# A two-layer encoder's seam between MLP and latent attention: a scratch pool of its own, two tiles' transposes moved among the latent products, and later weight splits tied to a later point

## The chip, the cores and the metric

The kernel runs on one core of one Trainium2 chip. The metric is the device time of one execution in microseconds, the median of several runs. A profile of one more execution gives the trace that is quoted here; times in it count from the start of its span.

## The reference

A bidirectional encoder of two layers works on 512 positions of width 1024 in float32. Each layer is x = x + mixer(norm(x)) followed by x = x + MLP(norm(x)). The MLP is squared ReLU, 1024 to 4096 to 1024. Layer 0's mixer is dilated window attention (A), layer 1's is multi-head latent attention (B):

```
lat = h @ w_in                                   # 1024 -> 256 + 128 + 64
q  = (rms_norm(lat[:256], g) @ w_qb)             # 8 heads of 128 + 64 (rotary)
kv = (rms_norm(lat[256:384], g) @ w_kvb)         # 8 heads of 128 (key) + 128 (value)
k  = concat(kv key part, lat[384:448] for all heads)
q, k = rms_norm per head, rotary on the last 64
y  = softmax(q k^T / sqrt(192)) v, all positions; then y @ w_o
```

The document is about the seam: the end of layer 0's MLP, the norm after it, the product `h @ w_in` ("the latents") and the first per-head products, up to the first attention scores.

## The kernel before

**Precision by splitting.** Every float32 product is made of three passes of a faster format: an operand x is split into a high part (ScalarE copies x to the short format, tile `whi` or the like) and a low part (VectorE computes x minus the high part, `wlo`). The product is high*high + high*low + low*high. So each weight tile costs a ScalarE instruction and a VectorE instruction before TensorE can use it, and so does each activation tile that TensorE has transposed.

**Tiles of positions.** The 512 positions are four tiles r = 0 to 3 of 128. The normed activations stand transposed in `hT` (eight blocks of 128 channels, high and low). A tile's path at the seam is in `norm_tile`: ScalarE squares and sums (L138), GpSimd raises to the power -1/2 (L133), VectorE multiplies by the row factor and by the gain table `g_mix` (L224, result `xn`), and then `turn` has TensorE transpose eight blocks in two halves (L125, tile `tp`), ScalarE write the high part into `hT` (L234) and VectorE the low part (L235).

**The end of the MLP** (`mlp`, `wino`) adds its products into `resid`. When both halves of a tile r are added, `done0(r, c)` is called and makes that tile's norm. Scratch there lives in the pool `mlp0`, where the pool's big tiles are the MLP's activations (`a2`) and sums (`S`); `xn` is in the same pool with tag `S`.

**The latents.** `run_block(w_units(b_w_in[0], 0, 448), [4], 448, ...)` makes, for each r in turn, 24 matmuls of 448 columns (four weight units u of two channel blocks, three passes) into the PSUM tile `acc` of that r. When a tile r is complete, `evac_lat(r, acc)` follows: three squares with sums on ScalarE into the scratch `junkb`, the power on GpSimd, VectorE's products with the gain table `gl` (result `cn`, L1009 and L1010), the rotary part, three transposes on TensorE into a `tp` tile, and `cT`, high by ScalarE (L1022), low by VectorE (L1023).

**The pairs.** The eight heads are worked in four pairs. `new_pair(p)` loads the pair's two weights (tile `raw`, three buffers, shared with all other weight loads) and splits them. `kv_chunk(d, r)` and `q_chunk(d, r)` project tile r of `cT`, evacuate, and return a second part that transposes the result. After the latents, the kernel runs the kv chunks of pair 0 and its first q chunk, then a loop of `score` steps into which later chunks are woven.

**What sets the order.** The kernel is written in the order above, but a scheduler that estimates times places each engine's instructions; each engine then runs its own list strictly in that order, and an instruction that waits holds up all that stand behind it. `tc.issue_after(ins)` adds an edge: what is created inside the block stands behind `ins` on the same engine. Loads are issued from SP's list, in its order. A tag with one buffer (the gain table's tag `gain` in pool `gp`, which holds `g_mix`, then `gl`, then `g_ffn`) makes the load of the next one wait until the last reader of the one before is done. PSUM tiles `tp` have two buffers.

`block_groups` has a hook that the MLP already uses: `between={i: f}` calls f after step i of the block; f's transposes stand behind step i's last matmul, and step i+1 stands behind f's last transpose. In the latents, step i is tile r = i // 4 and weight unit i % 4.

## Time and profile before

| | us |
|---|---|
| median of 3 runs | 1405.03 (1404.77 to 1405.65) |
| the profiled execution | 1405.79 |
| its span, first to last instruction | 1404.0 |
| TensorE busy in the span | 1371.9 (98%) |
| VectorE busy | 940.9 (67%) |
| ScalarE busy | 801.2 (57%) |
| GpSimd busy | 225.3 (16%) |
| mean granted TensorE clock | 0.999 |

In the views below, PE is TensorE, DVE VectorE, ACT ScalarE, POOL GpSimd and SPq the list from which SP issues loads. A row of the timeline has the start in us, the length in us, the engine, the line, the operation, the tiles (out<-in, buffer numbers left out), the shape, how many instructions were merged, and in brackets how long the engine was idle just before and what ended that. A length given for several merged matmuls is from the first one's start to the last one's end; matmuls overlap, so the step from one to the next is shorter than one's length.

The seam lies between 842 us (the last products of the MLP) and 904 us (the first score). The four latents run from 865.69 to 888.35 us, the first kv products start at 888.73 us, the first score matmul at 903.69 us, and the attention lasts until about 1005 us.

### The profile page before, as it was taken

What the parts mean: (1) busy time and instruction counts of PE and PEld (TensorE: products, weight loads), DVE (VectorE), ACT (ScalarE), POOL (GpSimd) and SP (SyncE); (2) the same over time, 40 slices, a digit from 0 to 9 for tenths busy, and PEclk for the clock granted to TensorE, in tenths of its full rate; (3) what the DMA queues carried; (4) which work ended last, traced back from release to release, by engine and by line L of the source; (5) the groups of instructions that cost most, each with busy time, mean ns of one, the idle gap of its engine ahead of it and who ended that gap; (6) DMA issues with size and microseconds to landing.
All of it is one profiled execution on the core that took longest, in us unless ns stands there. A gap on an engine that the chain in (4) does not pass through costs nothing.

```text
span 1404.0 us, 18978 instructions
## 1 busy us (share of the span) xinstructions
PE 1371.9 (98%) x6852; PEld 1164.1 (83%) x6852; DVE 940.9 (67%) x1498; ACT 801.2 (57%) x1643; POOL 225.3 (16%) x240
## 2 busy tenths in 40 slices
PE   7999999999999999999999999999999999999998
PEld 6999878888889989888888878777769888888886
DVE  6885777788788744574655769788745465574747
ACT  6543778687786625454536455777534553644543
POOL 1110212121122001020200204433201020020101
PEclk9999999999999999999999999999999999999999
DMA  9535554655555539486583944201116668493835
GB/s 301 172 133 162 131 135 98 164 124 133 143 125 123 159 106 260 142 187 176 121 238 86 235 96 94 61 31 31 46 46 191 170 132 228 100 226 124 200 85 120
DMA packets 171775, 197.83 MB, mean 141 GB/s; under 512 B 59105, under 2 KB 109025, under 8 KB 171681
## 3 DMA queue, kind: packets, MB, share of 16 engines
q1 hardware_dynamic: 152496, 157.55, 37.9%
q0 software_dynamic: 19184, 39.07, 15.5%
q8 instruction: 54, 0.88, 0.3%
q14 instruction: 41, 0.33, 0.1%
HBM read 176.13 MB, written 7.86 MB: 131 GB/s over the span
## 4 chain that ended last, share of the span: by engine, by line
PE 81%; DVE 7%; ACT 4%; DMA 4%; issue 2%; SPq 0%; POOL 0%; ACTq 0%; DVEq 0%
PE acc L188 46%; PE sc L868 11%; PE tp L868 7%; PE tp L125 3%; DMA xT<-t 2%; PE sc L430 2%; PE acc L1161 1%; PE sc L1055 1%; DVE wlo L811 1%; PE acc L1137 1%; PE tp L430 1%; PE sco L710 1%; PE acc L430 1%; PE sco L706 1%; ACT junk L138 1%
## 5 line engine op out<-in xcount | busy, mean ns | idle before, releaser
L188 PE MATMUL acc<-whi,hT 128*128 128x512 f32 (+2 forms) x1208 | 377.2, 388 | 1.9 <-ACT hT L752 1.0
L188 PE MATMUL acc<-hT_f,whi 128*128 128x512 f32 (+1 forms) x1152 | 317.4, 366 | 0.0
L159 DVE TENSOR_TENSOR wlo<-raw,whi 128x1024 fp32r<-128x1024 f32 (+3 forms) x146 | 172.9, 1188 | 164.3 <-ACT whi L158 163.7
L188 PEld LDWEIGHTS acc<-whi,hT 128*128 128x128 f32 x1208 | 224.3, 188 | 43.0 <-ACT hT L1163 1.5
L158 ACT ACTIVATE whi<-raw 128x1024 fp32r<-128x1024 f32 (+3 forms) x146 | 149.6, 1029 | 161.8 <-PE acc L188 72.1
L188 PEld LDWEIGHTS acc<-hT_f,whi 128*128 128x128 f32 x1152 | 207.8, 189 | 34.9
L188 PE MATMUL acc<-wlo,hT 128*128 128x512 f32 (+2 forms) x604 | 233.0, 387 | 0.7 <-DVE wlo L159 0.7
L811 DVE TENSOR_TENSOR wlo<-wqs,whi 128x1024 fp32r<-128x1024 f32 x112 | 137.7, 1231 | 112.9 <-ACT whi L810 112.9
L810 ACT ACTIVATE whi<-wqs 128x1024 fp32r<-128x1024 f32 x112 | 118.3, 1059 | 161.6 <-PE acc L188 65.0
L188 PE MATMUL acc<-hT_f,wlo 128*128 128x512 f32 (+1 forms) x576 | 204.1, 366 | 0.0
L868 PE MATMUL sc<-whi,asp 128*128 128x512 f32 x512 | 165.2, 390 | 1.3 <-DVE resid L842 1.3
L796 POOL DMA_DIRECT2D wqs<-in_ffn_w_dram x64 | 77.6, 1347 | 540.1 <-DVE wlo L811 358.3
L188 PEld LDWEIGHTS acc<-wlo,hT 128*128 128x128 f32 x604 | 113.6, 188 | 20.2 <-DVE wlo L159 1.1
L188 PEld LDWEIGHTS acc<-hT_f,wlo 128*128 128x128 f32 x576 | 108.3, 189 | 17.4
L868 PEld LDWEIGHTS sc<-whi,asp 128*128 128x128 f32 x512 | 96.2, 188 | 21.9 <-issue 2.1
L868 PE MATMUL tp<-whi,asp 128*128 128x512 f32 x352 | 112.2, 390 | 0.9 <-DVE resid L842 0.9
L133 POOL TENSOR_TENSOR qrs<-rs_v,nhalf 128x4 f32<-128x4 f32 x48 | 65.9, 1376 | 264.1 <-DVE rs_v L130 233.2
L868 PE MATMUL sc<-wlo,asp 128*128 128x512 f32 x256 | 99.7, 390 | 0.0
L304 ACT ACTIVATE qkT<-xT 128x1024 uint16<-128x1024 uint16 x48 | 56.4, 1182 | 42.1 <-DMA xT<-t 42.0
L868 PEld LDWEIGHTS tp<-whi,asp 128*128 128x128 f32 x352 | 66.1, 188 | 15.0 <-DVE resid L842 1.3
L868 PE MATMUL tp<-wlo,asp 128*128 128x512 f32 x176 | 68.2, 390 | 0.0
L138 ACT ACTIVATE junk<-acc 128x128 f32<-128x128 f32 x192 | 52.1, 272 | 10.7 <-PE acc L188 7.0
(236 smaller groups left out, 2187.2 us busy)
## 6 DMA issues: line engine op xcount, KB each, us to landing
wqs<-in_ffn_w_dram SPq DMA_DIRECT2D x80, 512.0 KB, 5.2
raw<-in_ffn_w_dram SPq DMA_DIRECT2D x64, 512.0 KB, 4.2
wqs<-in_ffn_w_dram POOLq DMA_DIRECT2D x64, 512.0 KB, 7.5
raw<-in_a_w_qkv_dram SPq DMA_DIRECT2D x96, 256.0 KB, 3.2
b<-in_a_w_qkv_dram SPq DMA_DIRECT2D x24, 384.0 KB, 5.7
vall<-vo POOLq DMA_DIRECT2D x24, 192.0 KB, 2.3
raw<-in_a_w_o_dram SPq DMA_DIRECT2D x8, 512.0 KB, 3.8
raw<-in_b_w_o_dram SPq DMA_DIRECT2D x8, 512.0 KB, 3.8
```

Of the source, the lines that this page charges most:

```text
L125: return PE.transpose(o, i, ident)
L133: G.tensor_tensor(out, v[:, :n], nhalf[:, :n], op=ALU.pow)
L138: A.activation(junk, x, AF.Square, scale=1.0 / math.sqrt(dim), accum_out=out)
L158: A.activation(hi[:, :nk, :n], raw[:, :nk, :n], AF.Copy)
L159: V.tensor_tensor(lo[:, :nk, :n], raw[:, :nk, :n], hi[:, :nk, :n].bitcast(F32), op=ALU.subtract)
L188: last = PE.matmul(accs[o][:, oc], lhsT=lt, rhs=rt, start=(kt == 0 and p_i == 0 and hv == 0), stop=(kt == total - 1 and p_i == 2), skip_gr ...
L304: A.activation(dst, xT.rearrange("p (h c) t -> p c t h", h=2), AF.Copy)
L430: PE.matmul(banks[t][:, :VH], lhsT=lt, rhs=rt[:, j], start=(first and k == 0 and i_ == 0), stop=(k == 3 and i_ == 2), skip_group_check=True)
L796: marks["sum"] = nc.gpsimd.dma_start(t, src, accum_op=ALU.add).ins
L810: A.activation(hi, x, AF.Copy)
L811: V.tensor_tensor(lo, x, hi.bitcast(F32), op=ALU.subtract)
L868: PE.matmul(bk[t], lhsT=lt, rhs=rt[:, j], start=(first and k == 0 and i_ == 0), stop=(k == 3 and i_ == 2), skip_group_check=True)
```

## The change

Four edits, all in layer 1's mixer and the norm ahead of it:

1. The scratch tiles `junkb`, `cn`, `kr2`, `qs`, `ks` and `pe` move from the pool `bw` to a new pool `bl`. Pool `bw` is left with the tiles that live longer. A tile that lies over addresses of an earlier pool waits for that pool's tiles, so the move alters which tiles of `mlp0` the scratch waits for.
2. `done0` makes the norm of tiles 2 and 3 but no longer transposes them; their `turn` functions are kept and called by the hook, between the latents' step 4 and 5, and step 8 and 9.
3. `new_pair(0)` stands ahead of the latents instead of behind them. The evacuation of the latents becomes `latent(r, acc)`: after `evac_lat(r)` it starts `kv_chunk(r - 1)` and finishes the one before. The last kv chunk and the first q chunk follow behind the latents.
4. `new_pair(p)` issues both loads first, and for p > 0 its splits stand behind the first Exp of the attention on ScalarE (`marks["exp", 0, 0]`) in that engine's list.

```diff
             if r == 0:
                 state["g"] = gain_table(norm_mix[1:2, :].rearrange("o d -> (o d)"), D, "g_mix1")
                 state["hT"] = new_hT()
-            norm_tile(r, resid[:, r], state["g"], state["hT"], mp, xn_tag="S")()
+            turn = norm_tile(r, resid[:, r], state["g"], state["hT"], mp, xn_tag="S")
+            if r < 2:
+                turn()
+            else:
+                state[f"turn{r}"] = turn
...
         with tc.tile_pool(name="bpool", bufs=1, reuse_waits="tile") as bp, \
+                tc.tile_pool(name="bl", bufs=2, reuse_waits="tile") as bl, \
                 tc.tile_pool(name="bw", bufs=2, reuse_waits="tile") as bw:
...
-                junk = bw.tile([P, QL], F32, tag="junkb", name=nm("junkb"), bufs=1)
+                junk = bl.tile([P, QL], F32, tag="junkb", name=nm("junkb"), bufs=1)
...
-                d["wkv"] = load_unit(wkv[:, :, 512 * p:512 * p + 512], 1, None, 512, home=homes[1])
-                d["wq"] = load_unit(wq[:, :, 384 * p:384 * p + 384], 2, None, 384, home=homes[0])
+                srcs = ("wkv", wkv[:, :, 512 * p:512 * p + 512], 1, 512), ("wq", wq[:, :, 384 * p:384 * p + 384], 2, 384)
+                raws = [load_raw(src, nk, None, n) for _, src, nk, n in srcs]
+                with ExitStack() as behind:
+                    if p:
+                        behind.enter_context(tc.issue_after(marks["exp", 0, 0]))
+                    for i, (name, src, nk, n) in enumerate(srcs):
+                        d[name] = load_unit(src, nk, None, n, home=homes[1 - i], raw=raws[i])
...
-                pe = bw.tile([P, S], F32, tag="pe", name=nm("pe"), bufs=3)
-                A.activation(pe, sc, AF.Exp, bias=mx[:, 1:2], scale=rq, accum_out=mx[:, 2:3])
+                pe = bl.tile([P, S], F32, tag="pe", name=nm("pe"), bufs=3)
+                marks["exp", h, r] = A.activation(pe, sc, AF.Exp, bias=mx[:, 1:2], scale=rq, accum_out=mx[:, 2:3]).ins
...
-            run_block(w_units(b_w_in[0], 0, 448), [4], 448, act_stationary(hT, 448), evac_lat)
-            oB = new_hT()
             cur = new_pair(0)
             late = []
-            for r in range(NT):
-                late.append(kv_chunk(cur, r))
-                if r == 2:
-                    late.append(q_chunk(cur, 0))
+
+            def latent(r, acc):
+                evac_lat(r, acc)
                 if r:
+                    late.append(kv_chunk(cur, r - 1))
+                if r > 1:
                     late.pop(0)()
+
+            run_block(w_units(b_w_in[0], 0, 448), [4], 448, act_stationary(hT, 448), latent,
+                      between={4: state["turn2"], 8: state["turn3"]})
+            oB = new_hT()
+            late += [q_chunk(cur, 0), kv_chunk(cur, NT - 1)]
```

How the lists move is not to be read from these lines. Three places follow; the number at the end of a tile's name is its buffer, and a bracket names the engines or loads that the instruction waits for. The number of instructions in each engine's list is the same or differs by a handful of waits; the work is the same.

The first place is TensorE's list where tile 0's latents end. Before, `xn_7639` is tile 2's normed activations, `acc_7713` and `acc_7714` are the latents of tiles 0 and 1:

```order
L188 MATMUL acc_7713<-whi_7737,hT_7516 128x448
L125 MATMUL tp_7646<-ck,xn_7639 128x128 [waits DVE_49]
L125 MATMUL tp_7646<-ck,xn_7639 128x128 x3
L188 MATMUL acc_7714<-whi_7719,hT_7516 128x448 x2
L188 MATMUL acc_7714<-wlo_7720,hT_7516 128x448
L188 MATMUL acc_7714<-whi_7719,hT_7516 128x448
L188 MATMUL acc_7714<-whi_7725,hT_7516 128x448
```

In the changed kernel, where `acc_7699`, `acc_7700` and `acc_7701` are the latents of tiles 0, 1 and 2, `cn_7761` is tile 0's scaled latent and `acc_7837` pair 0's first kv product:

```order
L188 MATMUL acc_7699<-whi_7723,hT_7516 128x448
L188 MATMUL acc_7700<-whi_7705,hT_7516 128x448 [waits DVE_49]
L188 MATMUL acc_7700<-whi_7705,hT_7516 128x448
L188 MATMUL acc_7700<-wlo_7706,hT_7516 128x448
L188 MATMUL acc_7700<-whi_7705,hT_7516 128x448
L125 MATMUL tp_7769<-ck,cn_7761 128x128 [waits DVE_49]
L125 MATMUL tp_7769<-ck,cn_7761 128x128
L125 MATMUL tp_7781<-ck,xn_7639 128x128 [waits PE_49]
L125 MATMUL tp_7781<-ck,xn_7639 128x128 x3
L125 MATMUL tp_7769<-ck,cn_7761 128x128 [waits DVE_49]
L1065 MATMUL acc_7837<-w_7687,cT 128x512 [waits Activation_49]
L1065 MATMUL acc_7837<-w_7687,cT 128x512
```

The transposes of tile 0's scaled latent, which stood behind nearly all the latents, now stand four matmuls behind the end of tile 0's, and tile 2's transposes and all later latents stand behind them.

The second place is VectorE's list at the same point. In the changed kernel `xn_7648` is tile 3's normed activations, the last reader of `g_mix`:

```order
L235 TENSOR_TENSOR hT_7516<-tp_7555,hT_7516 128x4x128 [waits Activation_49]
L130 TENSOR_SCALAR rs_v_7650<-nss_7647 128x1 [waits Activation_49]
L224 SCALAR_TENSOR_TENSOR xn_7648<-resid,nrs_7652,g_mix_1249_7514 128x1024 [waits Pool_49]
L130 TENSOR_SCALAR rs_v_7757<-lss_7752 128x2 [waits Activation_49]
L1011 TENSOR_SCALAR ssr<-ssr 128x1 [waits Activation_49]
L1014 SCALAR_TENSOR_TENSOR cn_7761<-acc_7699,lrs_7759,gl 128x256 [waits DMAHW5_49,PE_49,Pool_49]
L1015 SCALAR_TENSOR_TENSOR cn_7761<-acc_7699,lrs_7759,gl 128x128 [waits DMAHW6_49]
```

Before, the same stretch has a split of pair 0's weight ahead of tile 3's normed activations (there `xn_7662`) and the four low parts of tiles 2 and 3 behind it:

```order
L130 TENSOR_SCALAR rs_v_7664<-nss_7661 128x1 [waits Activation_49]
L159 TENSOR_TENSOR w_7712<-raw_7941,w_7712 128x2x384 [waits DMAHW1_49]
L224 SCALAR_TENSOR_TENSOR xn_7662<-resid,nrs_7666,g_mix_1249_7514 128x1024 [waits Pool_49]
L235 TENSOR_TENSOR hT_7516<-tp_7646,hT_7516 128x4x128 [waits Activation_49]
L235 TENSOR_TENSOR hT_7516<-tp_7653,hT_7516 128x4x128 [waits Activation_49]
L235 TENSOR_TENSOR hT_7516<-tp_7669,hT_7516 128x4x128 [waits Activation_49]
L235 TENSOR_TENSOR hT_7516<-tp_7676,hT_7516 128x4x128 [waits Activation_49]
```

The first `cn` now stands three rows behind the last reader of `g_mix`; its waits DMAHW5 and DMAHW6 are the two loads of `gl`, and SP's list issues them, as before, behind that last reader.

The third place is TensorE's list where tile 1's latents (`acc_7700`) end in the changed kernel. `cn_7823` is tile 1's scaled latent, `xn_7648` tile 3's normed activations, `acc_7916` pair 0's second kv product:

```order
L188 MATMUL acc_7700<-whi_7723,hT_7516 128x448
L1065 MATMUL acc_7837<-w_7687,cT 128x512 [waits DVE_49]
L188 MATMUL acc_7701<-whi_7705,hT_7516 128x448 x2
L188 MATMUL acc_7701<-wlo_7706,hT_7516 128x448
L188 MATMUL acc_7701<-whi_7705,hT_7516 128x448
L1065 MATMUL sc_8017<-w_7687,cT 128x384 x4
L125 MATMUL tp_7831<-ck,cn_7823 128x128 [waits DVE_49]
L125 MATMUL tp_7831<-ck,cn_7823 128x128
L125 MATMUL tp_7860<-ck,xn_7648 128x128 [waits PE_49]
L125 MATMUL tp_7860<-ck,xn_7648 128x128 x3
L125 MATMUL tp_7831<-ck,cn_7823 128x128 [waits DVE_49]
L1065 MATMUL acc_7916<-w_7687,cT 128x512 [waits Activation_49]
```

Before, tile 1's last latent is followed directly by tile 2's, and nothing of `evac_lat` stands there:

```order
L188 MATMUL acc_7714<-whi_7737,hT_7516 128x448
L188 MATMUL acc_7715<-whi_7719,hT_7516 128x448 [waits Activation_49]
L188 MATMUL acc_7715<-wlo_7720,hT_7516 128x448
L125 MATMUL tp_7669<-ck,xn_7662 128x128 [waits DVE_49]
L125 MATMUL tp_7669<-ck,xn_7662 128x128 x3
L188 MATMUL acc_7715<-whi_7719,hT_7516 128x448 x2
L188 MATMUL acc_7715<-wlo_7720,hT_7516 128x448
```

Now nine matmuls lie between the end of tile 1's latents and the first transpose of its scaled latent, and tile 3's transposes stand behind that one.

More of the change, by code (lines that the diff above doesn't have):

```diff
@@ L1007, in evac_lat @@
                 rs = rstd_of(ss[:, 0:2], 2, EPS, "lrs")
-                cn = bw.tile([P, QL + KVL], F32, tag="cn", name=nm("cn"))
+                cn = bl.tile([P, QL + KVL], F32, tag="cn", name=nm("cn"))
                 V.scalar_tensor_tensor(cn[:, 0:QL], acc[:, 0:QL], rs[:, 0:1], gl[:, 0:QL], op0=ALU.mult, op1=ALU.mult)
@@ L1011, in evac_lat @@
                                        op1=ALU.mult)
-                t2 = bw.tile([P, 2 * RD], F32, tag="kr2", name=nm("kr2"), bufs=1)[:, 0:RD]
+                t2 = bl.tile([P, 2 * RD], F32, tag="kr2", name=nm("kr2"), bufs=1)[:, 0:RD]
                 V.tensor_tensor(krr[:, r], acc[:, 384:448], cgB[:, r, 1], op=ALU.mult)
@@ L1062, in q_chunk @@
                 a3 = acc[:, :384].rearrange("p (h d) -> p h d", h=2)
-                junk = bw.tile([P, QL], F32, tag="junkb", name=nm("junkb"), bufs=1)
+                junk = bl.tile([P, QL], F32, tag="junkb", name=nm("junkb"), bufs=1)
                 ss = st.tile([P, 8], F32, tag="qss", name=nm("qss"))
@@ L1068, in q_chunk @@
                 rstd_of(ss[:, 0:2], 2, QKD * EPS, None, d["rq"][:, r])
-                qs = bw.tile([P, 2, DH], F32, tag="qs", name=nm("qs"), bufs=2)
+                qs = bl.tile([P, 2, DH], F32, tag="qs", name=nm("qs"), bufs=2)
                 A.activation(qs, a3[:, :, 0:DH], AF.Copy)
@@ L1101, in kv_chunk @@
                 a4 = acc.rearrange("p (h c d) -> p h c d", h=2, c=2)
-                junk = bw.tile([P, QL], F32, tag="junkb", name=nm("junkb"), bufs=1)
+                junk = bl.tile([P, QL], F32, tag="junkb", name=nm("junkb"), bufs=1)
                 ss = st.tile([P, 8], F32, tag="kss", name=nm("kss"))
@@ L1107, in kv_chunk @@
                 A.activation(d["v"][:, r], a4[:, :, 1], AF.Copy)
-                ks = bw.tile([P, 2, DH], F32, tag="ks", name=nm("ks"), bufs=2)
+                ks = bl.tile([P, 2, DH], F32, tag="ks", name=nm("ks"), bufs=2)
                 V.tensor_tensor(ks, a4[:, :, 0], rs.unsqueeze(2).broadcast_to([P, 2, DH]), op=ALU.mult)
```

## The prediction

> **What bounds the kernel now.** I read the page's chain of waits first, then the busy time by stretches around the seam, then the timeline of each engine there. The chain:
>
> ```profile
> PE 81%; DVE 7%; ACT 4%; DMA 4%; issue 2%; SPq 0%; POOL 0%; ACTq 0%; DVEq 0%
> ```
>
> TensorE's list sets the end. So a change is worth the idle time that it takes from or gives to TensorE, wherever it stands. The stretches (columns: length, busy time of PE, PE weight loads, DVE, ACT, POOL, each with its count, granted clock, DMA share, GB/s):
>
> ```profile
> 806.00:830.00 24.00, 24.00 (x108) 19.88 (x107) 10.67 (x10) 12.89 (x16) 0.00 (x0) 1.00 0.39 109
> 866.00:876.00 10.00, 10.00 (x58) 9.07 (x57) 8.50 (x11) 5.59 (x10) 0.55 (x1) 1.00 0.50 142
> 876.00:887.60 11.60, 11.60 (x62) 10.72 (x62) 6.39 (x22) 6.50 (x24) 2.72 (x5) 1.00 0.08 17
> 893.00:898.00 5.00, 3.69 (x20) 2.42 (x19) 4.63 (x19) 4.82 (x24) 4.82 (x9) 1.00 0.57 204
> 898.00:903.00 5.00, 3.46 (x24) 2.89 (x23) 3.73 (x15) 4.12 (x19) 3.72 (x7) 1.00 0.00 0
> 908.00:916.00 8.00, 6.67 (x35) 5.13 (x34) 6.97 (x21) 5.67 (x22) 2.63 (x4) 1.00 0.00 1
> 916.00:925.00 9.00, 9.00 (x59) 7.97 (x57) 8.76 (x29) 8.77 (x33) 3.38 (x5) 1.00 0.18 61
> 955.00:1003.00 48.00, 46.13 (x233) 34.79 (x232) 40.05 (x113) 34.01 (x111) 16.17 (x25) 1.00 0.11 32
> ```
>
> The reader is to see that TensorE is full through all four latents (866 to 887.6), loses 1.31 + 1.54 us between 893 and 903, 1.33 us between 908 and 916, and is nearly full in the attention behind (1.87 us of 48 idle from 955). The first score and the waits around it by name:
>
> ```profile
> 903.69 0.86 PE L1137 MATMUL acc<-kn,qn 128*128 128x512 f32 x3
> 894.46 0.33 PE L125 MATMUL tp<-ck,ks 128*128 128x128 f32 x1 [0.59 <-DVE ks L1109]
> 897.43 1.28 PE L1055 MATMUL sc<-w,cT 128*128 128x384 f32 x6 [0.59 <-DVE rs_v L130]
> 900.04 1.29 PE L1055 MATMUL sc<-w,cT 128*128 128x384 f32 x6 [0.89 <-DVE r L1076]
> 902.92 0.47 PE L1055 MATMUL sc<-whi,cT 128*128 128x512 f32 x1 [0.65 <-DVE rs_v L130]
> 912.17 0.51 PE L1137 MATMUL acc<-kn,qn 128*128 128x512 f32 x1 [0.24 <-DVE qn L1093]
> 913.76 0.96 PE L1137 MATMUL acc<-kn,qn 128*128 128x512 f32 x3 [1.08 <-ACT pe L1142]
> ```
>
> Four waits, 0.59 + 0.59 + 0.89 + 0.65 = 2.7 us, lie among the first kv and q chunks, two more, 1.3 us, at the first scores. **4.0 us is all that this change can win here**, and it reorders a stretch in which TensorE now loses nothing.
>
> **The change part by part.** The work is the same (same products, transposes, loads), so only waits count.
>
> *The new pool* (edit 1) adds no instruction. It lets tile 0's squares start when its latent is done, about 872, where they stood at 881.45 behind tile 3's last high part. That alone is free; what it does to the order is costed next.
>
> *The wait for the gain table* (edits 2 and 3). In the changed list the first transpose of tile 0's scaled latent `cn` stands four matmuls behind the end of tile 0's latents. `cn` reads `gl`; `gl` shares its one buffer with `g_mix`; the last reader of `g_mix` is tile 3's norm. The rows:
>
> ```profile
> 868.23 0.68 DVE L842 TENSOR_TENSOR resid<-resid,sc 128x512 f32<-128x512 f32 x1
> 869.49 1.05 ACT L138 ACTIVATE xn<-resid 128x1024 f32<-128x1024 f32 x1
> 871.69 0.37 PE L188 MATMUL acc<-whi,hT 128*128 128x448 f32 x1
> 880.92 6.90 PE acc L188 x34
> 868.83 0.69 DVE L159 TENSOR_TENSOR w<-raw,w 128x512 fp32r<-128x512 f32 x1
> 871.63 0.14 DVE L130 TENSOR_SCALAR rs_v<-nss 128x1 f32<-128x1 f32 x1
> 871.85 0.55 POOL L133 TENSOR_TENSOR nrs<-rs_v,nhalf 128x1 f32<-128x1 f32 x1 [5.86 <-DVE rs_v L130]
> 872.55 0.96 DVE L159 TENSOR_TENSOR w<-raw,w 128x768 fp32r<-128x768 f32 x1 [0.78 <-ACT w L158]
> 873.43 1.28 DVE L224 SCALAR_TENSOR_TENSOR xn<-resid,nrs,g_mix 128x1024 f32<-128x1024 f32 x1
> 874.73 0.55 SPq L980 DMA_DIRECT2D gl<-in_b_q_a_gain_dram  x1
> DMA to landing us min/median/max: 3.1/3.2/3.2
> 883.68 0.48 DVE L1009 SCALAR_TENSOR_TENSOR cn<-acc,lrs,gl 128x256 f32<-128x256 f32 x1
> ```
>
> The first two rows are tile 3's last addition and its square. The third is tile 0's last matmul, the fourth (from the chain in order of time) gives 6.90 / 34 = 0.20 us from one such matmul to the next. TensorE is thus done with tile 0 and the four matmuls at 871.69 + 5 x 0.20 = 872.7. Tile 3's norm: the two splits `w` leave VectorE's list here (edit 3 puts them into the MLP), so the sum's row at 871.63 comes between 0.6 us earlier and as now; the power ends at 871.8 to 872.4; the product, no longer behind the split at 872.55, runs 1.28 us to 873.1 to 873.7; SP issues `gl` at once, as it did at 874.73 behind the product's end at 874.71; 3.1 us pass from issue to landing (the row below it, of both `gl` loads); 0.48 us for `cn`. That is 876.8 to 877.4, so TensorE waits **4.1 to 4.7 us, I take 4.4**. Behind it stand tile 2's transposes and every later latent, and ScalarE and VectorE have nothing to do but wait for those. [...]
>
> *Evictions two deep.* Behind those transposes the first kv product waits for `cT`, which on ScalarE stands behind a half of tile 2's high part; at tile 1 it is the same with tile 3. The rows, with those of the chain that is needed next:
>
> ```profile
> 872.53 0.60 ACT L234 ACTIVATE hT<-tp 128x512 fp32r<-128x512 f32 x1
> 888.93 0.49 ACT L1022 ACTIVATE cT<-tp 128x384 fp32r<-128x384 f32 x1
> 881.45 0.38 ACT L138 ACTIVATE junkb<-acc 128x256 f32<-128x256 f32 x1
> 882.35 0.17 DVE L130 TENSOR_SCALAR rs_v<-lss 128x2 f32<-128x2 f32 x1
> 882.60 0.70 POOL L133 TENSOR_TENSOR lrs<-rs_v,nhalf 128x2 f32<-128x2 f32 x1 [10.20 <-DVE rs_v L130]
> ```
>
> 0.60 + 0.49, less 0.1 of overlap, is 1.0 us (0.9 to 1.1) twice: **2.0 us**.
>
> *Tile 1's scaled latent.* From the first square at 881.45 to the end of `cn` at 883.68 + 0.48 the chain of three engines takes 2.7 us; the last matmul is 0.37 long with a step of 0.20, so 2.9 us pass from TensorE's next issue. In the changed list a row on the kv product's sums stands ahead of this `cn` on VectorE and needs two more squares on ScalarE, up to 0.5 us more. TensorE has nine matmuls of 0.20 us or less meanwhile, 1.8 us. It waits 1.1 to 1.6, **1.3 us**. Tile 2's chain is covered by the 22 latent matmuls of tile 3, 4.5 us; without them it would cost as much.
>
> *Behind the last latents.* Two of four kv chunks have moved ahead; kv chunks 2 and 3 and the q chunks still follow, with the same links (`rs_v`, `ks`, `r`) as the four waits quoted. At best all 2.7 us vanish. Against it: the third kv product again waits behind two evictions (1.0), and tile 3's scaled latent needs a `tp` bank that is freed behind seven VectorE rows (about 1.0), with fewer kv products left to fill in. Range -2.7 to +2.0; the order repeats the links one by one, so I take the upper part, **+1.3**.
>
> *Splits held back* (edit 4). Before, pairs 1 and 2 were split while TensorE was full:
>
> ```profile
> 885.83 2.36 DVE L159 TENSOR_TENSOR wlo<-raw,whi 128x512 fp32r<-128x512 f32 x3
> 890.72 0.96 DVE L159 TENSOR_TENSOR wlo<-raw,whi 128x768 fp32r<-128x768 f32 x1 [0.47 <-ACT whi L158]
> ```
>
> These 3.3 us of VectorE (and as many instructions of ScalarE) now run behind the first Exp, where pair 1's first kv product needs them at once and where both engines are 8.8 of 9 us busy (916 to 925). Nothing to 3.3 us; TensorE is still full there, which covers part: **+1.5**, near the middle. Pair 0's splits go into the MLP, whose last up-projection (806 to 830) leaves VectorE 13 and ScalarE 11 us of 24 idle: nothing; uncovered they would cost their VectorE time, 0.69 + 0.96 = 1.7 us.
>
> Sum: 4.4 + 2.0 + 1.3 + 1.3 + 1.5 = 10.5 us. Against the profiled execution (1404.0 span, 1405.79 in all) that is 1416.3; the median of the runs is 0.76 lower, so **1415.5**. Bounds: 4.1 + 1.8 + 1.1 - 2.7 = 4.3 and 4.7 + 2.2 + 1.6 + 2.0 + 3.3 = 13.8, so 1409.3 to 1418.8.
>
> **The rivals.**
>
> *Faster: `gl` is there in time.* Then the seam loses nothing ahead of 888 and the 4.0 us of waits behind vanish: 1401. It decides at 872.7: `gl` must have landed by about 872. Tile 3's last addition ends at 868.23 + 0.68 = 868.9; square, sum, power and product (1.05 + 0.14 + 0.55 + 1.28) and 3.1 us cannot end ahead of 875.0. For: all other engines have room. Against: this floor.
>
> *Slower still: TensorE runs slow after the long wait.* The trace has one long idle time, at the start:
>
> ```profile
> 9.66 1.97 PE L125 MATMUL tp<-ck,xn 128*128 128x128 f32 x8 [9.66 <-DVE xn L370]
> 13.03 3.57 PE acc L430 x10
> 20.37 1.73 PE acc L430 x10
> 862.09 1.03 PE L125 MATMUL tp<-ck,xn 128*128 128x128 f32 x8
> ```
>
> Eight transposes take 1.97 us behind it and 1.03 at 862; ten matmuls 3.57 us at 13 and 1.73 at 20. So some 7 us ran at about half speed. If a wait of 4.4 us sets that off, the 3.5 us or so of work done in 7 us falls in part into waits that are there anyway: +2.5, 1418. Against: 4.4 is less than half of 9.66, and no other wait in the trace is near it. [...]
>
> *The back half recovers:* the 2.7 us vanish and the splits hide: 4.4 + 2.0 + 1.3 - 2.7 = +5.0, 1410. For: two kv chunks less there. Against: the links above.
>
> *The change does not do what it says:* the scratch did not hold tile 0's evacuation, and the lists run as before: 1405. Against: the changed list.
>
> **How the numbers follow.** Forecast 56%, slow TensorE 20%, back half recovers 15%, `gl` in time 5%, no effect 4%. The range 1408.5 to 1419.5 takes in the first three but for their edges. A measurement here can tell 0.2% (2.8 us) from no change: faster 5%, within 0.2% 4%, slower 91%.
>
> **What would show it.** A TensorE wait of 4 to 5 us right behind tile 0's latents that ends with `cn`, with `gl` issued at the end of tile 3's norm; waits of about 1 us for `cT` behind tiles 0 and 1; 1 to 1.5 us for tile 1's `cn`; the first score 8 to 10 us later than 903.7. I am wrong if the first transpose of `cn` runs by 874, if the first four old waits are gone without heirs, or if the attention takes the delay back.

## The result and the profile after

The change makes the kernel slower: 1421.44 us (median of 6 runs, 1419.35 to 1425.77) against 1404.90 us (6 runs, 1402.89 to 1406.95). The ratio, taken from all runs and not from the two medians, is 1.0123, 95% interval 1.0103 to 1.0142. The forecast was 1415.5 us with a range to 1419.5: the direction is right, the size is not, 16.5 us against 10.5. One execution of a later kernel, with `gl` early and pair 0 late, took 1980.36 us at a mean granted clock of 0.656 and is left out of that kernel's figures.

The profiled execution after the change took 1420.99 us, with a span of 1419.2 us against 1404.0: 15.2 us to account for. TensorE still sets the end; the chain of waits of the changed kernel, by engine:

```profile
PE 80%; DVE 7%; ACT 5%; DMA 5%; issue 2%; SPq 0%; POOL 0%; ACTq 0%; DVEq 0%
```

The stretch from the first latent to the first score, in the busy time by stretches (start and end, length, then busy time of PE, PE weight loads, DVE, ACT, POOL, granted clock, DMA share, GB/s), first of the kernel before:

```profile
865.69:903.69 38.00, 35.10 (x193) 30.61 (x191) 28.73 (x79) 26.16 (x92) 14.16 (x25) 1.00 0.34 98
```

and of the changed kernel:

```profile
867.52:916.96 49.44, 39.10 (x194) 33.40 (x192) 23.93 (x74) 22.56 (x86) 13.14 (x22) 0.90 0.10 29
```

These two rows divide the loss. The first latent starts 867.52 - 865.69 = 1.83 us later. The stretch is 11.44 us longer: TensorE idles 10.34 us in it instead of 2.90 (+7.44), and is busy 39.10 us instead of 35.10 **for the same work** (+4.00), at a granted clock of 0.90 instead of 1.00. From the first score to the end of the span it is 502.24 us instead of 500.31 (+1.93). 1.83 + 7.44 + 4.00 + 1.93 = 15.2. (The busy time of this stretch is itself uncertain: in the profiles of the kernel before, of its single edits and of the kernel one tile later, which have no half clock in it, it lies between 34.18 and 35.78 us, with 189 to 197 instructions.)

The idle time by name, in TensorE's timeline of the changed kernel:

```profile
867.52 0.36 PE L188 MATMUL acc<-whi,hT 128*128 128x448 f32 x1
878.46 0.44 PE L125 MATMUL tp<-ck,cn 128*128 128x128 f32 x2 [3.82 <-DVE cn L1014]
880.40 1.22 PE L1065 MATMUL acc<-w,cT 128*128 128x512 f32 x2 [0.96 <-ACT cT L1027]
890.12 0.44 PE L125 MATMUL tp<-ck,cn 128*128 128x128 f32 x2 [1.07 <-DVE cn L1014]
892.06 0.73 PE L1065 MATMUL acc<-w,cT 128*128 128x512 f32 x2 [0.96 <-ACT cT L1027]
904.62 0.73 PE L1065 MATMUL acc<-w,cT 128*128 128x512 f32 x2 [0.83 <-ACT cT L1027]
906.28 0.55 PE L125 MATMUL tp<-ck,cn 128*128 128x128 f32 x3 [0.92 <-DVE cT L1028]
910.27 0.45 PE L125 MATMUL tp<-ck,ks 128*128 128x128 f32 x1 [1.22 <-DVE ks L1119]
915.64 0.30 PE L125 MATMUL tp<-ck,ks 128*128 128x128 f32 x1 [0.45 <-DVE rs_v L130]
916.96 0.49 PE L1147 MATMUL acc<-kn,qn 128*128 128x512 f32 x1
```

The wait of 3.82 us is the forecast one. VectorE's timeline shows tile 3's product and, behind it, `cn` waiting for a load:

```profile
873.33 1.28 DVE L224 SCALAR_TENSOR_TENSOR xn<-resid,nrs,g_mix 128x1024 f32<-128x1024 f32 x1 [0.67 <-POOL nrs L133]
877.92 0.48 DVE L1014 SCALAR_TENSOR_TENSOR cn<-acc,lrs,gl 128x256 f32<-128x256 f32 x1 [2.64 <-DMA gl<-in_b_q_a_gain_dram]
```

and SP's timeline the issue, at the end of that product (873.33 + 1.28):

```profile
874.64 0.33 SPq L985 DMA_DIRECT2D gl<-in_b_q_a_gain_dram  x1
```

The 4.00 us of slower work have their own rows. The stretches below are 3.41 us long and lie on one grid (each boundary is 16.33 us, where the clock first rises in this execution and the step from one matmul of 384 columns to the next falls from 0.32 to 0.17 us, plus a multiple of 3.413); the second column is TensorE's busy time, the third from the end the granted clock:

```profile
842.36:845.77 3.41, 1.58 (x7) 1.31 (x8) 3.41 (x5) 1.06 (x1) 0.19 (x1) 1.00 0.09 17
873.08:876.49 3.41, 1.56 (x8) 1.11 (x6) 1.61 (x3) 1.16 (x6) 0.92 (x2) 1.00 0.34 83
876.49:879.90 3.41, 0.98 (x7) 0.75 (x7) 1.08 (x5) 0.53 (x2) 0.32 (x1) 1.00 0.20 40
879.90:883.31 3.41, 2.91 (x9) 2.54 (x10) 1.16 (x2) 0.45 (x2) 0.00 (x0) 0.50 0.02 5
903.80:907.21 3.41, 1.67 (x9) 1.16 (x10) 2.27 (x9) 1.50 (x4) 0.78 (x2) 1.00 0.31 118
907.21:910.62 3.41, 2.19 (x8) 1.26 (x7) 2.50 (x10) 3.31 (x18) 1.66 (x3) 0.50 0.09 36
910.62:914.03 3.41, 3.41 (x15) 3.31 (x14) 1.64 (x7) 2.06 (x9) 3.41 (x6) 0.50 0.00 0
```

The clock is either 1.00 or 0.50 for the whole of each of these stretches. It falls behind 876.49 to 879.90, in which TensorE was busy 0.98 us, and again behind 903.80 to 907.21, in which it was busy 1.67 us and **idle for no more than 0.92 us in a row**. If half of the busy time at half speed is lost, that is (2.91 + 2.19 + 3.41) / 2 = 4.26 us, about the 4.00 found above.

The 1.83 us ahead of the first latent: TensorE's wait for the residual in the MLP's last tiles, before

```profile
842.39 0.50 PE L868 MATMUL tp<-whi,asp 128*128 128x512 f32 x1 [0.92 <-DVE resid L842]
```

and after:

```profile
844.19 0.50 PE L868 MATMUL tp<-whi,asp 128*128 128x512 f32 x1 [2.12 <-DVE resid L842]
```

1.20 us of the 1.83 are this wait. 0.2 us are scatter: the residual's addition ahead of all that differs starts at 802.07 and 802.28. The rest collects in smaller waits between. The wait comes from further back. ScalarE's timeline of the changed kernel:

```profile
808.13 0.63 ACT L158 ACTIVATE w<-raw 128x512 fp32r<-128x512 f32 x1 [9.32 <-DMA raw<-in_b_w_kvb_dram]
821.93 1.06 ACT L810 ACTIVATE whi<-wqs 128x1024 fp32r<-128x1024 f32 x1 [6.46 <-DMA wqs<-in_ffn_w_dram]
822.90 0.58 ACT L907 ACTIVATE a<-acc 128x512 f32<-128x512 f32 x1
```

and SP's, first before,

```profile
810.54 5.81 SPq L798 DMA_DIRECT2D wqs<-in_ffn_w_dram  x2
```

then after:

```profile
809.52 0.37 SPq L148 DMA_DIRECT2D raw<-in_b_w_qb_dram  x1
815.81 1.50 SPq L798 DMA_DIRECT2D wqs<-in_ffn_w_dram  x2
```

Pair 0's loads stand ahead of the MLP's last weight loads on SP, which go out from 815.81 instead of 810.54. On ScalarE pair 0's split and then the MLP's own wait for loads, and the activation `a` behind them starts at 822.90; before it started at

```profile
820.66 0.60 ACT L907 ACTIVATE a<-acc 128x512 f32<-128x512 f32 x1 [0.53 <-PE acc L188]
```

VectorE's last idle time ahead of the seam's additions ends at 825.62 us before and at 827.42 after, 1.80 us later; from there on it is full (24.00 of 24 us from 830 to 854, in both kernels), so that the residual can't catch up.

### The profile page after: what moved, and what is told of

Same layout as the page of the kernel before. It is cut to its first block, busy times and chain, and to the rows that moved or that the text cites. A ratio compares the mean times of both kernels' runs of the same rounds, so it can differ in the third digit from the quotient of the medians.

```text
span 1419.2 us, 18974 instructions
## 1 busy us (share of the span) xinstructions
PE 1378.4 (97%) x6852; PEld 1166.2 (82%) x6852; DVE 939.2 (66%) x1498; ACT 801.2 (56%) x1643; POOL 225.9 (16%) x240
## 4 chain that ended last, share of the span: by engine, by line
PE 80%; DVE 7%; ACT 5%; DMA 5%; issue 2%; SPq 0%; POOL 0%; ACTq 0%; DVEq 0%
PE acc L188 46%; PE sc L868 10%; PE tp L868 7%; PE sc L430 3%; PE tp L125 3%; DMA xT<-t 3%; PE acc L1171 1%; DVE wlo L811 1%; PE acc L1147 1%; PE tp L430 1%; PE sc L1065 1%; PE acc L430 1%; PE sco L710 1%; PE sc L596 1%; PE sco L706 1%
```

## The experiments

My theory after the profile was the sum of the prediction plus two things that it had at nothing: the half clock, and the delay at the MLP's end by pair 0's splits. The rivals: that the half clock fell into waits and cost nothing, that the waits only move when `gl` is early, and that each edit's price is its own and adds up. Every run is compared with the kernel before on the same chip (1405.6 to 1405.9 us there); the runs were on three chips, and the kernel before has medians from 1404.90 to 1405.89 us in all, so a difference between two runs is good to about 1 us at best.

### The gain table in time, and pair 0's splits back in their old place

Three kernels: `gl` in a buffer of its own; pair 0's loads and splits behind the latents' weights; both.

```
-            gl = gp.tile([P, D], F32, tag="gain", name="gl")
+    gl = res_p.tile([P, QL + KVL], F32, name="gl")        # ahead of the MLP; its loads are issued at 501.3 us
```
```
-            cur = new_pair(0)
             def latent(r, acc):
+                if r == 0:
+                    first.append(new_pair(0))
                 evac_lat(r, acc)
```

> The changed kernel with one thing different: the gain table gl has a place of its own and is loaded long before the seam, so the scaled latent of tile 0 waits for no load. All engines' lists are as in the changed kernel. Theory (the long wait costs its own 3.8 us and sets off the first stretch at half clock, 879.9 to 883.3, in which 2.9 us of TensorE work took twice its time, so up to 1.5 us): the wait shrinks to what the chain of tile 0's scaled latent leaves, about 0.7 us, the stretch is gone, 1421.4 - 3.1 - 1.5 = 1416.8; if the second stretch at half clock (907.2 to 914.0, up to 2.8 us) is a follower of the first, 1414. Rival 1 (the half clock falls into waits and costs nothing): 1418.3. Rival 2 (the wait only moves to the evictions behind it): 1420 to 1421.5.

Measured: 1420.97 us, ratio 1.0113 (1.0095 to 1.0131), the time of the change. The theory's 1416.8 is missed, and the time is inside rival 2's 1420 to 1421.5. TensorE's timeline:

```profile
881.90 0.44 PE L125 MATMUL tp<-ck,cn 128*128 128x128 f32 x2 [1.66 <-DVE cn L1014]
```

The wait did not fall to 0.7 us but to 1.66, and the clock still fell twice behind it (a matmul of 448 columns at 884.86 is 0.58 us long instead of 0.36, a transpose at 911.02 0.42 instead of 0.27). In this execution (1425.25 us, the slowest of four) the clock had also halved twice at the MLP's end (matmuls of 512 columns at 846.23 and 860.21 are 0.63 us long instead of 0.39).

> The changed kernel with pair 0's weights loaded and split where the kernel before has them, behind the latents' weights; TensorE's list is unchanged, on VectorE and ScalarE the two splits leave the MLP's last tiles. Theory (these splits cost the MLP's end 1.8 us): the first latent starts 1.8 us sooner than in the changed kernel, and the TensorE wait for the residual of 2.1 us falls back to 0.9. In the total hardly any of it: the second split stands ahead of tile 3's product again, gl is issued at the same time as in the changed kernel, and the wait for gl takes the 1.8 us up: 1420.5 to 1421.5, with a wait of about 5.5 us there. Rival (the total follows the MLP's end): 1419.6. Rival (the MLP's end was late for another reason): first latent unchanged.

Measured: 1421.01 us, ratio 1.0108 (1.0093 to 1.0123). As the theory had it, which expected a wait of about 5.5 us: the residual's wait is back at 0.93 us and the first latent at 866.27 us, and the wait for `gl` takes it all up, since the transposes behind it start at 878.38 us instead of 878.46:

```profile
878.38 0.69 PE L125 MATMUL tp<-ck,cn 128*128 128x128 f32 x2 [4.99 <-DVE cn L1014]
```

> Both edits together: gl loaded early and pair 0's splits where the kernel before has them. Theory (the 1.8 us of the MLP's end are real and only the wait for gl hides them): 1.8 us below the kernel with gl loaded early alone, 1415.0 if that is 1416.8, and first latent as early as in the kernel before. Rival (the MLP's end was late for another reason): no difference between the two.

Measured: 1418.80 us, ratio 1.0093 (1.0076 to 1.0110), 2.2 us below the kernel with `gl` early alone. That is near the 1.8 us expected of the difference, but the two intervals overlap, and the 1415.0 us expected of the time is missed. TensorE still waits for `cn`, with `gl` there:

```profile
876.50 0.44 PE L125 MATMUL tp<-ck,cn 128*128 128x128 f32 x2 [2.90 <-DVE cn L1014]
```

VectorE's timeline of the same kernel tells why:

```profile
873.78 1.28 DVE L224 SCALAR_TENSOR_TENSOR xn<-resid,nrs,g_mix 128x1024 f32<-128x1024 f32 x1
874.98 0.16 DVE L130 TENSOR_SCALAR rs_v<-lss 128x2 f32<-128x2 f32 x1
875.96 0.48 DVE L1014 SCALAR_TENSOR_TENSOR cn<-acc,lrs,gl 128x256 f32<-128x256 f32 x1 [0.76 <-POOL lrs L133]
```

Tile 0's own chain (squares, sum, power, product) stands behind tile 3's norm on VectorE. So `gl` was worth 4.99 - 2.90 = 2.1 us of the wait; the other 2.9 us come from where the transposes of `cn` stand, four products behind the latents that they hang on, as the next experiment tests.

### The transposes one tile later

On the last kernel, what TensorE does with a scaled latent is moved one tile down the program:

```
             def latent(r, acc):
-                evac_lat(r, acc)                      # with transposes of cn, cT
+                turned.append(evac_lat(r, acc))       # squares, power, cn
+                if r:
+                    turned[r - 1]()                   # transposes of cn, cT
-                if r:  late.append(kv_chunk(first[0], r - 1))
-                if r > 1:  late.pop(0)()
+                if r > 1:  late.append(kv_chunk(first[0], r - 2))
+                if r > 2:  late.pop(0)()
             ...                                       # the chunks behind the last latent, in the same manner
```

> The kernel with gl loaded early and pair 0's splits late (1419.2), with one thing different: what TensorE does with a tile's scaled latent (transposes, cT) and the kv product stand one tile later in the program, behind the next tile's latents. Theory (what cost most was the place of these transposes, four products behind the sums that they hang on, so that the chain of three engines lay bare, with or without gl): the waits for cn (2.9 + 1.1) and two of the waits for cT (0.96 each) go, and the first stretch at half clock with them, 1.6 us: 1419.2 - 5.9 - 1.6 = 1411.7; 1410 if the second stretch goes too. Rival (the waits only move to the kv chunks behind the last latents): 1416 to 1419.

Measured: 1409.39 us, ratio 1.0024 (1.0014 to 1.0034): 3.8 us above the kernel before on its chip, where the last kernel was 12.9 us above it. The stretch from first latent to first score:

```profile
865.77:905.43 39.66, 35.24 (x193) 30.41 (x191) 25.57 (x76) 23.61 (x88) 14.17 (x24) 1.00 0.16 48
```

No wait for `cn` behind tiles 0 and 1 is left, TensorE idles 4.42 us instead of 9.51, and its busy time is that of the kernel before: no half clock. This is the largest single effect of all runs. Of the 3.8 us that are left in its profiled execution (a span of 1407.8 us), 1.5 are idle time in this stretch and 2.1 come behind the first score (502.37 us to the end, instead of 500.31).

### The clock by itself

The changed kernel with its waits filled by products whose sums nobody reads; in the second kernel six short ones more behind each of three tiles' transposes (only the first edit is shown):

```
             def latent(r, acc):
+                if r == 0:
+                    spare = sc_p.tile([P, 512], F32, tag="sc", name=nm("spare"))
+                    with tc.issue_after(marks["last"]):        # tile 0's last latent
+                        for i in range(16):
+                            PE.matmul(spare, lhsT=hT[:, i % 8, 0, 0:P], rhs=hT[:, 0:4, 0, 0:P], ...)
```

> The changed kernel with 16 products of the normed tile 0, whose sums nobody reads, added to TensorE's list right behind tile 0's last latent: 16 x 0.23 = 3.6 us, just less than the 3.82 us that TensorE stood there waiting. The wait for gl is as long as before, only TensorE is busy in it; so this prices the clock by itself. Theory (half clock costs time): no stretch at half clock behind this place, 1421.4 - 1.5 = 1419.9, and 1417 if the second stretch goes too. Rival (the half clock falls into waits and costs nothing): 1421.4, or up to 0.5 more where the products outlast the wait.

Measured: 1419.38 us, ratio 1.0097 (1.0080 to 1.0114). That is nearer to the theory's 1419.9 than to the rival's 1421.4, but the interval overlaps with that of the change (1.0103 to 1.0142) and doesn't tell them apart. In the profiled execution the clock fell once instead of twice, behind tile 1 (a mean of 0.97 from first latent to first score, against 0.90).

> The changed kernel with the 16 products in the wait for gl (as in the kernel with the filled wait), and 6 more short ones, 128 columns each, behind the transposes of the scaled latents of tiles 0, 1 and 2, where TensorE waits 0.96, 0.96 and 0.83 us for cT; nobody reads their sums. No wait of the other engines changes. Theory (what counts for the clock is how much of a stretch of 3.41 us TensorE is busy, and below about half of it the next one runs at half clock): with these waits filled too no stretch at half clock is left from the first latent to the first score, in most executions, and the time falls below the 1419.4 of the filled wait, to 1417.5 to 1418.5. Rival (only a long wait sets it off, and the second stretch follows from the first): as the filled wait alone, 1419.4, or later by what the products outlast the waits, up to 1 us.

Measured: 1418.73 us, ratio 1.0090 (1.0076 to 1.0104), 0.2 us above the range of the theory and below the rival. The stretch from first latent to first score has no half clock:

```profile
867.33:914.62 47.29, 41.15 (x228) 35.54 (x226) 24.23 (x74) 22.94 (x87) 13.73 (x24) 1.00 0.10 32
```

The added work is not free: where TensorE waited 3.82 us it now works and waits longer,

```profile
873.48 3.81 PE L1190 MATMUL spare<-hT 128*128 128x512 f32 x16
878.31 0.44 PE L125 MATMUL tp<-ck,cn 128*128 128x128 f32 x2 [0.20 <-DVE cn L1015]
```

and over the stretch idle time and added products together are 6.14 + 5.51 = 11.65 us against 10.34 idle (5.51 is an estimate from the timeline: the next product starts 3.65 us behind the first of the 16, and each six end 0.62 us later than the transposes ahead of them). So the half clock did not fall into waits: this kernel is not slower but faster, although TensorE does more. How much the clock gave back is less certain. By the medians it is 2.7 us, or 3.4 with each kernel against the kernel before on its own chip, and the 1.3 us by which the products outlast the waits have to be added: 4.0 to 4.7 us. By the busy time of the two profiles it is 39.10 - (41.15 - 5.51) = 3.5 us. The intervals of the change and of this kernel just touch (1.0103 and 1.0104), so all of these are good to about 2 us; the 4.0 of the account lies among them. What the short products bring alone (0.7 us between the two kernels) is within the uncertainty.

### Edits alone

Edit 1 alone, the pool `bl`, on the kernel before:

```
+                tc.tile_pool(name="bl", bufs=2, reuse_waits="tile") as bl, \
-                junk = bw.tile([P, QL], F32, tag="junkb", ...)
+                junk = bl.tile([P, QL], F32, tag="junkb", ...)      # and cn, kr2, qs, ks, pe
```

> The kernel before with edit 1 alone: the scratch of the seam in the new pool bl. Theory (the buffers add no instruction, and the time comes from the order that they make possible with edits 2 and 3): no change, 1404 to 1406.5, first latent to first score within 1 us of the 38.0 us before. Rival (the four waits of 2.7 us behind the latents came from the scratch): 1402 to 1403. Rival (the pool itself costs, by pushing other tiles): above 1407.

Measured: 1405.78 us, ratio 1.0003 (0.9994 to 1.0012). No effect, as expected.

Pair 0 early alone, on the kernel before:

```
+            cur = new_pair(0)
             run_block(w_units(b_w_in[0], 0, 448), [4], 448, act_stationary(hT, 448), evac_lat)
-            cur = new_pair(0)
```

> The kernel before with pair 0's weights loaded and split ahead of the latents, alone; nothing else of the change. Theory (the splits delay the residual's additions in the MLP's last tiles): the first latent starts 1.8 us later than at 865.7 and the wait for the residual there grows from 0.9 to about 2 us, while the seam behind it gains up to 1 us from the two splits that are done: 1406 to 1407.5, and more in executions in which the MLP's end falls to half clock. Rival (VectorE had room there, as the prediction said): first latent at 865.7, 1404.5 to 1405.5.

Measured: 1407.15 us, ratio 1.0014 (1.0004 to 1.0024), but its twelve executions lie between 1404.72 and 1412.04. The stretches at the MLP's end of the profiled one (1410.78 us):

```profile
841.05:844.46 3.41, 1.39 (x6) 0.88 (x6) 3.41 (x4) 1.06 (x1) 0.00 (x0) 1.00 0.24 43
844.46:847.87 3.41, 3.41 (x9) 2.65 (x9) 3.20 (x4) 1.31 (x2) 1.20 (x1) 0.50 0.26 14
854.70:858.11 3.41, 1.33 (x6) 0.75 (x5) 3.41 (x5) 1.22 (x2) 1.65 (x1) 1.00 0.00 0
858.11:861.53 3.42, 3.23 (x8) 2.61 (x9) 2.98 (x5) 2.30 (x4) 0.36 (x1) 0.50 0.01 2
```

VectorE (third busy column) is full, TensorE waits 2.02 and 2.27 us for the residual, and that is enough to halve the clock twice; with it the first latent comes at 871.69 us, 6.0 later than before, where the theory had 1.8. In the profile of the changed kernel the same place had 1.58 us busy and kept its clock. The stretches lie differently in each execution (a boundary at 841.05 us here, at 842.36 in the changed kernel), which fits the wide spread: the four executions above 1409 us had a mean granted clock of 0.997 to 0.998, the eight below it 0.999 to 1.000.

Edit 4 alone, the splits of pairs 1 and 2 held back:

```
+                with ExitStack() as behind:
+                    if p:
+                        behind.enter_context(tc.issue_after(marks["exp", 0, 0]))
```

> The kernel before with edit 4 alone: the splits of pairs 1 and 2 held back behind the first Exp. In the changed kernel 498.2 us pass from the first score to the end, 496.0 in the kernel before. Theory (that is edit 4): 1405.5 + 2.2 = 1407.7, lost in the attention at the pairs' ends, with the first score not later than before. Rival (the attention's loss follows from the changed order ahead of it): 1405.5. The prediction's step had +1.5.

Measured: 1408.90 us, ratio 1.0024 (1.0016 to 1.0033): 3.3 us, more than the 2.2 expected. (The 498.2 and 496.0 us of the expectation count to TensorE's last product, the 502.24 and 500.31 above to the end of the span.) In its profile the stretch from first latent to first score is 0.8 us shorter, with 189 instructions of TensorE in place of 193, and from the first score to the end it is 504.28 us, 4.0 more than before. Two waits at the pairs' ends, which the kernel before does not have, are 1.7 of these:

```profile
955.08 3.70 PE L1166 MATMUL acc<-pTs,vb 128*128 128x512 f32 x8 [0.63 <-ACT pTs L1158]
988.53 1.98 PE L1166 MATMUL acc<-pTs,vb 128*128 128x512 f32 x4 [1.07 <-ACT pTs L1158]
```

Other waits went in turn: TensorE's idle time behind the first score grew by only 0.5 us (11.31 against 10.81), its busy time by 3.5 (492.97 against 489.50). Part of that are the four instructions; the rest stays open.

### Do the prices add up?

The changed kernel and the kernel one tile later, each without edit 4:

```
-                    if p:
+                    if False:
                         behind.enter_context(tc.issue_after(marks["exp", 0, 0]))
```

> The changed kernel without edit 4: the splits of pairs 1 and 2 are issued as early as their loads allow. The lists behind the latents are planned anew. Theory (edit 4's cost is its own and adds up): 1421.2 - 3.3 = 1417.9, with 496 us from the first score to the end. Rival (the order that edits 2 and 3 leave needs the splits held, since VectorE would do them ahead of the chains of the scaled latents and of the sums): the attention gains 2 us and the stretch ahead of the first score loses as much, 1420.5 to 1422.

Measured: 1423.40 us, ratio 1.0126 (1.0112 to 1.0140), 5.5 us above the theory and above the rival's range too.

> The kernel with everything one tile later (1409.4) without edit 4. Theory (costs add up): 1409.4 - 3.3 = 1406.1, as the kernel before. Rival (without the hold the splits stand ahead of the chains on VectorE): 1409 to 1411, with waits for cT of 1.5 to 2 us behind the last latents.

Measured: 1412.79 us, ratio 1.0055 (1.0041 to 1.0069), 3.4 us slower than with edit 4, and again above the rival's 1411. So the theory of prices that add up falls: **edit 4, which costs 3.3 us alone, earns 3.4 us in the kernel one tile later.** In the changed kernel the medians differ by 2.0 us the same way, but the intervals of the ratios overlap almost wholly (1.0103 to 1.0142 with it, 1.0112 to 1.0140 without); what is shown there is that it does not cost its 3.3 us. The stretch from first latent to first score of the kernel one tile later without edit 4:

```profile
864.84:909.42 44.58, 38.64 (x196) 34.08 (x195) 29.15 (x84) 26.71 (x94) 16.22 (x25) 0.92 0.27 79
898.46 0.75 PE L1068 MATMUL acc<-w,cT 128*128 128x512 f32 x2 [1.35 <-ACT cT L1029]
905.12 1.62 PE L1068 MATMUL sc<-w,cT 128*128 128x384 f32 x6 [2.15 <-DVE r L1089]
```

With edit 4 it was 39.66 us, with 4.42 idle and 35.24 busy. Of the 4.92 us more, 1.52 are idle time and 3.40 busy time. The clock, which kept 1.00 there with edit 4, fell twice, and both stretches at half clock are busy throughout: (3.41 + 3.41) / 2 = 3.41. So most of what edit 4 earns in this stretch is the clock. Behind the first score it costs 1.5 us (502.37 against 500.86). VectorE's timeline of the changed kernel without edit 4 shows what lengthens the waits:

```profile
904.41 0.22 DVE L130 TENSOR_SCALAR rs_v<-kss,ssr 128x2 f32<-128x2 f32 x1
904.53 1.68 DVE L159 TENSOR_TENSOR wlo<-raw,whi 128x768 fp32r<-128x768 f32 x2
906.81 0.42 DVE L1119 TENSOR_TENSOR ks<-acc,krs 128x256 f32<-128x256 f32 x1 [0.59 <-POOL krs L133]
```

and TensorE's:

```profile
908.91 1.27 PE L1065 MATMUL acc<-w,cT 128*128 128x512 f32 x3 [1.73 <-ACT cT L1027]
```

The splits of later pairs stand between the links of the chains that TensorE waits for; on ScalarE, too, a split (906.81 to 907.65 us, itself behind a load) stands ahead of the high part `cT` at 908.36. In the kernel before they stood at 885.83 and 890.72 us, where TensorE still had products to work off (busy 5.36 of 5.40 us from 887.60 to 893.00).

Last, the kernel one tile later with the transposes of normed tiles 2 and 3 where the kernel before has them:

```
-            if r < 2:
-                turn()
-            else:
-                state[f"turn{r}"] = turn
+            turn()
-                      between={4: state["turn2"], 8: state["turn3"]})
```

> The kernel with everything one tile later (1409.4) without the hooks of edit 2: the transposes of the normed tiles 2 and 3 stand where the kernel before has them, among the latents of tile 0. Theory (what the place of these transposes costs is the two evictions in a row on ScalarE): the wait of 0.96 us for cT behind tile 1's latents goes: 1407.5 to 1408.5. Rival (the order does not matter any more): 1409.4.

Measured: 1408.40 us, ratio 1.0025 (1.0015 to 1.0035), inside the theory's range of time but not told apart from 1.0024. The wait of 0.96 us for `cT` is down to 0.35, but two others are new, and in this profile the clock fell twice (a mean of 0.95 from first latent to first score):

```profile
896.07 0.52 PE L125 MATMUL tp<-ck,cn 128*128 128x128 f32 x3 [1.92 <-DVE kr L1136]
902.99 0.30 PE L125 MATMUL tp<-ck,ks 128*128 128x128 f32 x1 [1.66 <-DVE ks L1119]
```

None of the twelve kernels is faster than the kernel before, and nothing in them points to one that would be.

## Why the prediction was right in sign and wrong in size

The prediction's terms against the profiled execution:

| Step | Forecast | Measured |
|---|---|---|
| Wait for the gain table | 4.4 | 3.82 |
| Evictions two deep | 2.0 | 0.96 + 0.96 = 1.92 |
| Tile 1's scaled latent | 1.3 | 1.07 |
| Behind the last latents | +1.3 | 0.83 + 0.92 + 1.22 + 0.45 - 2.72 = +0.7 |
| Splits held back (all of the attention) | 1.5 | 1.93 |
| Pair 0's splits in the MLP | 0 | 1.2 + 0.4 = 1.6 (1.83 with scatter) |
| Slow clock | a rival at 20%, +2.5 | 4.0 (3.5 to 4.7 by the filled waits) |
| Sum | 10.5 | 15.2 |

The five terms of the sum came to 9.4 us against 10.5. **Two steps failed.**

*"Pair 0's splits go into the MLP ...: nothing."* The splits did run where the quoted row has VectorE free, at 808.80 and 813.61 us. The step counted their 1.7 us of VectorE and not what else was moved with them: two loads on SP ahead of the MLP's last two, and two instructions on ScalarE that wait for those loads with the MLP's own activation behind them in the list. Free time in a stretch was taken for free places in a list. That the 1.7 us given as the uncovered price is near what was measured is chance; alone on the kernel before it measured 1.6 us in the median, and 5 us in the profiled execution that lost its clock. In the changed kernel this step moved time and did not add any that the runs can tell: with pair 0's splits back in their old place the total is the same, 1421.01 us, and the wait for `gl` is 4.99 us, 0.6 more than the 4.4 forecast. So it is the other step that carried the time past the forecast. With the clock held by the filled waits the time is 1418.73 us, inside the forecast range.

*The slow clock as a rival.* The step weighed one wait of 4.4 us by its own length, beside the 9.66 us of the start, and gave it 20%. That the clock falls only behind one long idle time is shown by no run. What the runs showed in its place: the boundaries lie on a grid of 3.413 us to within 0.01 us, and the clock fell behind stretches with 0.98 and with 1.67 us of work in 3.41, in the second with no idle time over 0.92 us. So no wait has to fill such a stretch: several short ones were enough there, and the waits that this sum had forecast were enough by themselves. In the profiles of the changed kernel and of all variants that keep its order, the clock fell between first latent and first score, once to three times (a mean of 0.84 there without edit 4, 0.90 in the changed kernel, 0.97 with the long wait filled); only with most of the waits filled it held (1.00). It should have been a term of the sum: with the 4.0 us measured, the forecast would have been 14.5 us above the kernel before, 1419.5. Of the 2 us that are still missing 1.3 are the choice of the profiled executions: they are 15.2 us apart, the medians 16.5.

Two terms were near in size but their reason was not the whole. The gain table is 2.1 us of its wait; with it in time the wait was still 2.9 us, so that the first rival ("`gl` is there in time", 1401) was wrong too: it asked when `gl` lands and not when tile 0's own chain ends. And the attention's 1.93 us are not what edit 4 costs in all, as the table's row may suggest: without edit 4 the changed kernel is not faster. Nor are they waits, as the step had it: TensorE's idle time behind the first score is 10.65 us against 10.81 before, and its busy time 491.59 against 489.50, which no run here explains.

Of the signs that the prediction named, the issue of `gl`, the waits for `cT` and tile 1's wait came as said, and the wait behind tile 0 with 3.82 us just under the 4 to 5 named. The first score came 13.3 us later than 903.69 and not 8 to 10: 7.4 from waits, 1.8 at the MLP's end, 4.0 from the clock.

## What to carry to other kernels

Where TensorE's list is full, moving dependent work closer behind its producer lays the chain of the other engines bare; count the products that stand between the sum and the first instruction that hangs on it, and compare them with the chain's length (here four, 0.8 us, against 2.7 us; one tile later these waits were gone). When a forecast puts waits into a stretch of a few us, add up TensorE's busy time there as well: in the changed kernel the clock fell to 0.50 behind stretches of 3.41 us with 0.98 and 1.67 us of work and held behind two with 1.56 and 1.58, and half speed cost it 4.0 us. A load that is moved up can cost time on the queue that issues it and on an engine whose list waits for it, even where that engine has idle time: here the MLP's last loads went out from 815.81 us instead of 810.54, and ScalarE's activation behind them started at 822.90 instead of 820.66. The price of an edit measured alone does not tell its price beside others: holding the splits back cost 3.3 us alone and earned 3.4 us in the kernel one tile later.

## What was not expected of the hardware

The clock's windows. In the profile of the changed kernel the clock was 1.00 or 0.50 for whole stretches of a grid of 3.413 us: from its first rise at 16.33 us it kept 1.00 for 253 of them, then 0.50 for one (879.90), 1.00 for seven and 0.50 for two (907.21). The grid lies differently in each execution (in the kernel before the clock first rises at 16.69 us). In the changed kernel it fell behind stretches in which TensorE was busy 0.98 and 1.67 us (0.29 and 0.49 of the stretch), and held behind two with 1.56 and 1.58 us (0.46). Busy time alone does not separate them: in the rows above 1.56 us of products only (873.08) held, and 1.67 us with six transposes among nine instructions (903.80) fell. What else tells them apart no run here tested by itself; a stretch with 1.51 us of products only fell too (gl early alone, 842.54; a matmul of 512 columns behind it is 0.63 us long instead of 0.39). Behind the stretch at half clock that was busy 2.19 us (907.21) the clock stayed at half; behind those with 2.91 (879.90) and 3.41 us (910.62) it rose again. Since the grid lies differently in each execution, a kernel with stretches as busy as these should spread more: 1404.7 to 1412.0 us with pair 0's splits early (12 executions), against 1403.8 to 1408.1 for the kernel before (32 on the same chip). Not every spread is the clock's: with edit 1 alone it is 1404.5 to 1408.9, the slowest at a mean granted clock of 1.000.
